# Loading the last tile in two halves and storing it in pieces of 4, 2, 1 and 1 rows

## The chip, the cores and the metric

The kernel runs on one NeuronCore of one Trainium2 chip. The metric is device time in microseconds (us), the median of several executions.

## The reference

`x` has the shape (32, 512, 2048), float32. The last axis is split in two halves of 1024, and the result is gelu(first half) times second half, float32:

```python
half_dim = x.shape[-1] // 2
x1, x2 = (x[..., :half_dim].copy(), x[..., half_dim:].copy())
gelu_x1 = 0.5 * x1 * (1 + erf(x1 / np.sqrt(2)))
return (gelu_x1 * x2).astype(np.float32)
```

That is 134.22 MB read and 67.11 MB written, with little arithmetic per byte.

## The kernel before

The 16384 rows are cut into 16 tiles of 128 partitions x 8 rows. ACT (ScalarE) applies gelu in place to one row per partition, DVE (VectorE) multiplies it into an output tile. Two input and two output buffers rotate. Loads go through the queue of the sync engine (SP), stores through ACT's queue, except those of the last tile, which go through SP's queue in four pieces of two rows, so that storing can begin before all eight rows are done.

```python
R = 8
x_t = x_flat.rearrange("(n p r) d -> n p r d", p=P, r=R)
o_t = out_flat.rearrange("(n p r) d -> n p r d", p=P, r=R)
...                                           # cut: pools with bufs=2 each
def load(i):
    x_tile = xpool.tile([P, R, dim], x.dtype, name="x_tile")
    nc.sync.dma_start(out=x_tile, in_=x_t[i])
    return x_tile

ahead = [load(0), load(1)]
for i in range(n_tiles):
    x_tile = ahead.pop(0)
    o_tile = opool.tile([P, R, half], out.dtype, name="o_tile")
    last = i == n_tiles - 1
    pieces = 4 if last else 1
    step = R // pieces
    for k in range(pieces):
        for r in range(k * step, (k + 1) * step):
            ...                               # cut: gelu on ACT, multiply on DVE
        rows = slice(k * step, (k + 1) * step)
        queue = nc.sync if last else nc.scalar
        queue.dma_start(out=o_t[i][:, rows, :], in_=o_tile[:, rows, :])
    if i + 2 < n_tiles:
        ahead.append(load(i + 2))
```

## Time and profile before

| | before |
|---|---|
| time, median of 3 runs | 472.24 us (471.88 to 472.3) |
| span of the profiled run | 470.3 us |
| DVE / ACT busy | 31% / 26% |
| bytes moved, mean rate | 201.35 MB, 428 GB/s |

These lines are from the page of the kernel before: busy time by engine, then the DMA rows of the 40-slice picture (a 9 is 90% or more), then the chain of work that ended last, by line.

```profile
DVE 146.7 (31%) x128; ACT 124.2 (26%) x129; POOL 0.2 (0%) x4
...
DMA  8999999999999999999999999999999999999998
...
DMA x_tile<-in_x_dram 81%; DVE o_tile L55 15%; ACT x_tile L52 2%; DVEq L90 0%; SPq L40 0%; ACTq L52 0%
...
out_dram<-o_tile SPq DMA_DIRECT2D x4, 1024.0 KB, 5.6
```

The DMA engines are busy from the first slice to the last; the compute engines are idle most of the time. The last line, from the list of DMA issues, says that the four pieces of the last tile took 5.6 us from issue to landing, in the median.

Now the tail. The first fence is the timeline from 450 us (start, length, engine, operation; in brackets the idle time before it and what ended it). The second is the table of stretches (the stretch and its length, busy time of DVE, ACT and POOL, then the granted clock, the mean busy share of the 16 DMA engines, GB/s). Transfers are counted where they start, so a short stretch can show a share a little above 1 or below it.

```profile
453.23 7.68 ACT L52 ACTIVATE x_tile<-x_tile 128x1024 f32<-128x1024 f32 x8 [21.34 <-DMA x_tile<-in_x_dram]
454.32 9.17 DVE L55 TENSOR_TENSOR o_tile<-x_tile 128x1024 f32<-128x1024 f32 x8 [19.85 <-ACT x_tile L52]
456.70 7.14 SPq L62 DMA_DIRECT2D out_dram<-o_tile  x4
```

```profile
452.00:456.00 4.00, 1.68 (x2) 2.77 (x3) 0.00 (x0) 1.00 0.97 418
456.00:458.00 2.00, 2.00 (x3) 2.00 (x4) 0.00 (x0) 1.00 1.07 422
458.00:462.00 4.00, 4.00 (x4) 2.91 (x4) 0.00 (x0) 1.00 0.89 348
462.00:466.00 4.00, 1.49 (x2) 0.00 (x0) 0.00 (x0) 1.00 1.01 428
```

The last load lands, then ten microseconds of ACT and DVE work follow, with stores trickling out behind. The DMA engines stay full while that compute runs.

The records of single packets in the trace show why. A packet is one partition's contiguous run: 64 KB for a full load (median 2.418 us), 32 KB for a full store (1.213 us), 8 KB for a two-row piece (0.309 us). While both queues have work, each of the 16 DMA engines alternates between a load packet and a store packet. (The records don't name the engine, but a packet that starts where another ends can be matched to it. Of the 85 packets that start between 424 and 434 us, 76 have a clear successor, and it is always of the other queue.) When the last load's final packets end, the store of the tile before still has packets until 459.0, and the pieces follow at once until 469.0.

### The profile page before, as it was taken

Reading aid. Unit: us, or ns where it says so; the run is one execution under the profiler, and the core shown is the slowest. Engines: PE = TensorE matmul, PEld = TensorE weight load, DVE = VectorE, ACT = ScalarE, POOL = GpSimd, SP = SyncE. Lnnn points to the kernel's source line nnn. Section 1 sums busy time; section 2 is a strip of 40 time slices with the busy share of each in tenths; the row PEclk is TensorE's granted clock in tenths of the full one; section 3 lists DMA queues with packets and bytes.
Section 4 is the critical chain, followed back from the end, with each engine's and each line's share of the span. In section 5 each row is a group of like instructions: output and inputs, shape, how many; then the busy total and the mean of one; then the engine's idle time right before and its main releaser. Section 6 shows DMA issues by size and latency. Waiting matters only on the chain.

```text
span 470.3 us, 408 instructions
## 1 busy us (share of the span) xinstructions
DVE 146.7 (31%) x128; ACT 124.2 (26%) x129; POOL 0.2 (0%) x4
## 2 busy tenths in 40 slices
DVE  0070704307042070520606116060250702407034
ACT  1050605106050150601406024060330603206042
POOL 0000000000000000000000000000000000000000
DMA  8999999999999999999999999999999999999998
GB/s 357 446 446 382 429 443 424 463 404 443 426 446 421 443 415 449 413 443 424 457 429 435 438 438 415 426 438 435 440 440 418 449 438 435 424 443 432 418 410 351
DMA packets 5042, 201.35 MB, mean 428 GB/s; under 512 B 560, under 2 KB 560, under 8 KB 560
## 3 DMA queue, kind: packets, MB, share of 16 engines
q1 hardware_dynamic: 2880, 138.41, 68.4%
q10 hardware_dynamic: 2160, 62.92, 31.0%
q14 instruction: 2, 0.02, 0.0%
HBM read 134.22 MB, written 67.11 MB: 428 GB/s over the span
## 4 chain that ended last, share of the span: by engine, by line
DMA 81%; DVE 15%; ACT 2%; DVEq 0%; issue 0%; SPq 0%; ACTq 0%
DMA x_tile<-in_x_dram 81%; DVE o_tile L55 15%; ACT x_tile L52 2%; DVEq L90 0%; SPq L40 0%; ACTq L52 0%
## 5 line engine op out<-in xcount | busy, mean ns | idle before, releaser
L55 DVE TENSOR_TENSOR o_tile<-x_tile 128x1024 f32<-128x1024 f32 x128 | 146.7, 1218 | 316.8 <-ACT x_tile L52 316.8
L52 ACT ACTIVATE x_tile<-x_tile 128x1024 f32<-128x1024 f32 x128 | 122.9, 1042 | 336.0 <-DMA x_tile<-in_x_dram 336.0
L52 ACT ACT_TABLE_LOAD x1 | 1.3, 1283 | 0.7 <-PEq L79 0.7
L79 POOL MEMSET const-bfloat16-1.0<- 128x1 bf16 x1 | 0.1, 102 | 0.0
L79 POOL MEMSET const-uint8-127<- 128x1 uint8 x1 | 0.1, 102 | 0.0
L79 POOL MEMSET const-float32-1.0<- 128x1 f32 x1 | 0.1, 99 | 0.0
L79 POOL MEMSET const-float32-0.0<- 128x1 f32 x1 | 0.1, 98 | 0.2 <-issue 0.2
## 6 DMA issues: line engine op xcount, KB each, us to landing
out_dram<-o_tile ACTq DMA_DIRECT2D x15, 4096.0 KB, 39.4
out_dram<-o_tile SPq DMA_DIRECT2D x4, 1024.0 KB, 5.6
x_tile<-in_x_dram SPq DMA_DIRECT2D x16, 47.6
```

Of the source, the lines that this page charges most:

```text
L52: nc.scalar.activation(out=x_tile[:, r, :half], in_=x_tile[:, r, :half], func=GELU)
L55: nc.vector.tensor_mul(out=o_tile[:, r, :], in0=x_tile[:, r, :half], in1=x_tile[:, r, half:],)
L79: nc = _bacc.Bacc("TRN2", target_bir_lowering=False, num_devices=1)
```

## The change

Its intent: rows 0 to 3 of the last tile can be computed and issued while rows 4 to 7 are still arriving, so less work follows the last landing, and the very last store is only one row.

```diff
     def load(i):
         x_tile = xpool.tile([P, R, dim], x.dtype, name="x_tile")
-        nc.sync.dma_start(out=x_tile, in_=x_t[i])
+        parts = 2 if i == n_tiles - 1 else 1
+        for k in range(parts):
+            rows = slice(k * R // parts, (k + 1) * R // parts)
+            nc.sync.dma_start(out=x_tile[:, rows, :], in_=x_t[i][:, rows, :])
         return x_tile
...
-        pieces = 4 if last else 1
-        step = R // pieces
-        for k in range(pieces):
-            for r in range(k * step, (k + 1) * step):
+        cuts = [4, 6, 7, 8] if last else [8]
+        begin = 0
+        for end in cuts:
+            for r in range(begin, end):
...
-            rows = slice(k * step, (k + 1) * step)
+            rows = slice(begin, end)
             queue = nc.sync if last else nc.scalar
             queue.dma_start(out=o_t[i][:, rows, :], in_=o_tile[:, rows, :])
+            begin = end
```

## The prediction

> **What bounds the kernel now.** The page has the DMA engines nine tenths busy in every slice, 428 GB/s; DVE is busy 31%, ACT 26%. The chain of waits is 81% input loads. In the packet records of the trace a load runs as one 64 KB packet per partition (2.42 us each), a full store as 32 KB packets (1.21 us), a two-row piece as 8 KB packets (0.309 us). Each of the 16 engines takes load and store packets strictly in turn, so loads get two thirds. The Trainium skill says so ("DMA: Bandwidth & Descriptors", Queues, rings and completion order: round robin between queues, a whole packet at a time); the trace agrees: 10.03 MB of loads to 5.14 MB of stores between 400 and 435 us.
>
> **The tail before.** The last load lands at 453.14. ACT and DVE (1.15 us a row) work until 463.49; pieces are issued every 2.3 us from 456.70. These 17 us are not idle: the last tile but one still has store packets on each engine until about 458.5, and the pieces follow without a gap at 427 GB/s until 468.9. The span ends at 470.3. So after 453 us the tail is bound by bytes, not by the landing.
>
> **What the change does.** No byte is removed. One load issue is added (0.33 us of the sync queue, hidden). Rows 0 to 3 (5.7 us of ACT and DVE) move ahead of the second half's landing. It also halves the last load's packets to 32 KB, so I expect loads to get a half instead of two thirds while stores are queued. The first half then lands near 443, but the second near 459, six microseconds later than the whole tile now; the store of the last tile but one lands near 457 instead of 459.4. The four-row piece is computed by 449 but waits in the same queue behind the second half; it then gives 2.1 MB, 4.9 us, of cover from 458.5. The next piece needs landing, one ACTIVATE, two DVE rows and issue to first packet (about 1.2 us): 459.2 + 1.1 + 2.3 + 1.3 = about 464, when the cover has just run out: an idle gap of 0.5 to 1 us. The 4 KB packets of the one-row pieces cost 0.16 us each by estimate (half of 0.309). Data should end near 469.2 instead of 468.9.
>
> **On the critical path.** The compute taken from the tail (5 us) is already covered by DMA work: the gain is nil, the loss a small gap, 0.3 us.
>
> **Prediction.** 472.5 us, range 471.5 to 473.5. Faster by over 2%: 0.005; within 2%: 0.99; slower by over 2%: 0.005.
>
> **What would show each step.**
> - Turn-taking: between 424 and 440 us the DMA view has about equal megabytes on both queues.
> - The second half lands at 458 to 460 in the timeline (ACT's last four rows start there).
> - DVE's last row ends near 465, later than now.
> - DMA busy until 469, with at most one short dip near 464.
>
> **What would make it wrong.** If engines shared by bytes, or kept two to one with smaller packets, the second half would land near 453, no gap would appear, and the end could be 0.3 us earlier. If issue to first packet took 2 us for the late pieces, the gap would grow and cost 1 us. Slower one-row packets move the end by tenths. Nothing here reaches 2%.

## The result, and the profile after

A ratio is the mean time of one kernel's fast runs over that of the other's of the same rounds, so it is not quite the ratio of the medians quoted.

| | before | after |
|---|---|---|
| median, first comparison | 472.27 us (4 runs) | 472.74 us (4 runs, 472.41 to 473.45) |
| ratio, 95% interval | | 1.0012 (0.9995 to 1.003) |
| span of the profiled run | 470.3 us | 471.3 us |

There is no gain, and no loss that the interval can tell from nothing. These are the page's lines after:

```profile
DVE 146.9 (31%) x128; ACT 124.3 (26%) x129; POOL 0.2 (0%) x4
...
DMA  8999999999999999999999999999999999999997
...
out_dram<-o_tile SPq DMA_DIRECT2D x1, 2048.0 KB, 17.2
out_dram<-o_tile SPq DMA_DIRECT2D x1, 1024.0 KB, 3.9
out_dram<-o_tile SPq DMA_DIRECT2D x2, 512.0 KB, 4.1
```

The timeline and the stretches after, as above:

```profile
442.21 3.90 ACT L56 ACTIVATE x_tile<-x_tile 128x1024 f32<-128x1024 f32 x4 [9.26 <-DMA x_tile<-in_x_dram]
443.30 4.63 DVE L59 TENSOR_TENSOR o_tile<-x_tile 128x1024 f32<-128x1024 f32 x4 [7.77 <-ACT x_tile L56]
447.96 18.56 SPq L66 DMA_DIRECT2D out_dram<-o_tile  x4
460.31 3.90 ACT L56 ACTIVATE x_tile<-x_tile 128x1024 f32<-128x1024 f32 x4 [14.21 <-DMA x_tile<-in_x_dram]
461.40 4.63 DVE L59 TENSOR_TENSOR o_tile<-x_tile 128x1024 f32<-128x1024 f32 x4 [13.47 <-ACT x_tile L56]
```

```profile
458.00:462.00 4.00, 0.60 (x1) 1.69 (x2) 0.00 (x0) 1.00 0.93 397
462.00:466.00 4.00, 4.00 (x4) 2.21 (x3) 0.00 (x0) 1.00 0.63 266
```

The intent was met in one respect: rows 0 to 3 are done at 447.93 and only four rows follow the last landing. But that landing moved from 453.1 to 460.3 us. (In this profile the whole chain was already 1.06 us late when the last load was issued, at 406.56 instead of 405.50, before anything changed; the repeat below is without that.) The four-row piece, issued at 447.96, needed 17.2 us to land, because it lies in the same queue behind the second half of the load. And the DMA engines now have a hole: share 0.63 between 462 and 466, where it was 1.01.

Why the landing moved is seen in the bytes per queue between 424 and 434 us. The columns are packets, MB, and share of the 16 engines' time; q1 is SP's queue (here loads), q10 is ACT's (stores). First before, then after:

```profile
q1 hardware_dynamic: 44, 2.88, 66.5%
q10 hardware_dynamic: 41, 1.34, 31.1%
```

```profile
q10 hardware_dynamic: 74, 2.42, 56.1%
q1 hardware_dynamic: 66, 2.10, 48.5%
```

Before, loads got two thirds; after, about a half. The half-tile load has 32 KB packets, as the store has, and the engines take turns by packets. The total did not change; the load merely arrives later, and the store that runs beside its first half earlier: that of the last tile but two lands at 437.3 instead of 444.9 us. All 138 data packets that start in these ten microseconds after the change are followed by one of the other queue.

### The profile page after: what moved, and what is told of

It reads as the page before. It is cut to its first block, busy times and chain, and to the rows that moved or that the text cites. A ratio compares the mean times of both kernels' runs of the same rounds, so it can differ in the third digit from the quotient of the medians.

```text
span 471.3 us, 411 instructions
## 1 busy us (share of the span) xinstructions
DVE 146.9 (31%) x128; ACT 124.3 (26%) x129; POOL 0.2 (0%) x4
## 4 chain that ended last, share of the span: by engine, by line
DMA 78%; DVE 14%; another core or an unknown queue 3%; ACT 3%; DVEq 0%; issue 0%; SPq 0%; ACTq 0%
DMA x_tile<-in_x_dram 78%; DVE o_tile L59 14%; ACT x_tile L56 3%; DVEq L95 0%; SPq L44 0%; ACTq L56 0%
## 6 DMA issues: line engine op xcount, KB each, us to landing
out_dram<-o_tile SPq DMA_DIRECT2D x1, 2048.0 KB, 17.2
```

## The experiments

The theory: (1) the tail is bound by bytes, so compute after the landing costs nothing as long as the DMA engines have something queued; (2) smaller load packets shift the turn-taking and delay the second half; (3) after that landing, the queued four-row piece covers about 4.9 us, and the next piece's packets come about then or a little later, which leaves a hole. Rivals: the compute after the landing is on the path after all; small pieces or the extra DMA cost time in themselves; the difference is chance.

"Idle" in this section is worked out from the packet records: the length of a stretch less the summed packet durations in it divided by 16 engines. Recorded packets overlap slightly, so a full stretch comes out a little below zero. Four columns for each run: idle from 450 to 466 us, idle from 466 us to the last data, time of the last data (all us, one profile each), and the median time with the number of timed runs.

```
                idle 450-466   idle 466-end   last data   median (runs)
before             -0.11           0.32         469.0     472.27 (4)
after               1.42           0.02         469.9     472.74 (4)
r_again             0.63           0.03         469.2     472.24 (5)
a_load_only         0.93           0.06         469.5     472.36 (5)
b_store_only        1.66           0.02         470.2     473.29 (5)
c_two_to_one       -0.13           1.07         469.4     472.04 (5)
d_one_row          -0.14           0.65         469.0     472.16 (5)
l_four_four         2.70           0.23         471.2     474.17 (5)
h_fast_tail        -0.12           0.62         469.0     472.19 (5)
k_seven_rows       -0.05           0.45         466.7     469.79 (5)
e_both             -0.17           0.98         469.3     472.17 (5)
```

The kernel before was timed beside each group, on the same chip: median 472.31 us for r, a, b and c; 472.35 for d, h, k and l; 472.32 for e. The three groups ran on three chips, so runs of different groups are compared by their ratio to the kernel before. The profiled execution is not always a typical one: that of a_load_only and that of c_two_to_one were the slowest of their five.

### r_again: the changed kernel once more

No edit.

> The changed kernel again, to narrow its interval beside the others. My theory (bytes bound, plus an idle gap of the DMA engines of about 1.4 us on average after the second half's landing): 0.5 to 1.0 us above the kernel before, gap seen again between 462.5 and 465. Rival (the difference is chance between runs): 0 within 0.3 us, and no stable gap.

Measured: 472.24 us beside 472.31, ratio 0.9999 (0.9987 to 1.0012). The expected 0.5 to 1.0 us of loss did not appear; in the time, chance within 0.3 us is the better reading, and the 0.47 us of the first comparison must not be called a measured loss. The hole is there again, but smaller. ACT starts the last four rows at 459.61. The stretches 458 to 462 and 462 to 466:

```profile
458.00:462.00 4.00, 1.30 (x2) 2.39 (x3) 0.00 (x0) 1.00 0.97 414
462.00:466.00 4.00, 3.33 (x3) 1.51 (x2) 0.00 (x0) 1.00 0.81 336
```

In the first profile the last load packet ended between 456.7 and 459.9 us depending on the engine; here between 458.0 and 459.2. The landing waits for the slowest engine, while the idle is on the engines that were done first. So a run in which the engines have drifted further apart has the larger hole. a_load_only, below, lies between the two (456.9 to 459.7 us, idle 0.93). That is read from three profiles, not tested.

### h_fast_tail: is the compute after the landing on the path?

The kernel before, with a wrong result.

```diff
-                nc.scalar.activation(
-                    out=x_tile[:, r, :half], in_=x_tile[:, r, :half], func=GELU
-                )
+                if last and r % 2 == 0:
+                    nc.scalar.activation(
+                        out=o_tile[:, r, :], in_=x_tile[:, r, :half], func=GELU
+                    )
+                    continue
+                if not last:
+                    nc.scalar.activation(
+                        out=x_tile[:, r, :half], in_=x_tile[:, r, :half], func=GELU
+                    )
```

> The kernel before, with a wrong result on purpose: in the last tile even rows are only activated on ACT and odd rows only multiplied on DVE, so the eight rows take about 5 us instead of 10.3 after the landing. My theory (the tail is bound by bytes): pieces are issued every 1.2 us from about 454.5, all are queued early, the end moves by less than 0.3 us. Rival (the compute after the last landing is on the critical path, which the change set out to shorten): 5 us earlier, ratio 0.989.

The timeline shows that the compute did shrink, and the list of DMA issues shows what became of it:

```profile
453.57 3.90 ACT L53 ACTIVATE o_tile<-x_tile 128x1024 f32<-128x1024 f32 x4 [21.37 <-DMA x_tile<-in_x_dram]
453.58 4.63 DVE L61 TENSOR_TENSOR o_tile<-x_tile 128x1024 f32<-128x1024 f32 x4 [18.81 <-DMA x_tile<-in_x_dram]
454.89 5.08 SPq L68 DMA_DIRECT2D out_dram<-o_tile  x4
```

```profile
out_dram<-o_tile SPq DMA_DIRECT2D x4, 1024.0 KB, 9.0
```

DVE ends at 458.21 instead of 463.49, over five microseconds sooner, and the time is 472.19 us beside 472.35, ratio 0.9998 (0.9984 to 1.0012). What the compute gave up, the pieces spent waiting in the queue: 9.0 us from issue to landing instead of 5.6. The rival's 5 us are excluded: the interval leaves at most 0.8 us. Even this much less compute after the landing, about what the change set out to save, is worth nothing here that these runs can resolve.

### k_seven_rows: do bytes count?

The kernel before; the last load brings seven rows, and row 7 is computed from row 6 (wrong).

```diff
-        nc.sync.dma_start(out=x_tile, in_=x_t[i])
+        rows = slice(0, 7 if i == n_tiles - 1 else R)
+        nc.sync.dma_start(out=x_tile[:, rows, :], in_=x_t[i][:, rows, :])
...                                # cut: ACT and DVE read row 6 for row 7
```

> The kernel before, with a wrong result on purpose: the last load brings 7 of 8 rows, and row 7 is computed from row 6, so compute and stores stay and 1.05 MB of load go. My theory (bytes bound): 1.05 MB at 433 GB/s, that is 2.4 us earlier, less 0.3 to 1 us if the compute after the landing then starts to show. Rival (latency of the compute chain after the landing alone): the landing itself comes earlier by as much, so this run tells only together with the fast tail run; bytes bound needs 2 us here and nothing there.

Measured: 469.79 us beside 472.35, ratio 0.9948 (0.9936 to 0.9961): 2.56 us between the medians. The 1.05 MB left out take 2.4 us at 433 GB/s (16 engines, 64 KB in 2.418 us). With the run before, this settles the first point: taking away compute gave nothing, taking away bytes gave their full time.

### a_load_only and b_store_only: each half of the change alone

```diff
 # a_load_only, against the changed kernel
-        cuts = [4, 6, 7, 8] if last else [8]
+        cuts = [2, 4, 6, 8] if last else [8]
```

> Load in halves kept, stores in four pieces of two rows as before. My theory: second half lands at 459 to 460 as in the changed kernel, two pieces wait behind it and give the same 4.9 us of cover, the third is issued at the same time as the changed kernel's second, so the gap of 1.4 us stays; end within 0.2 us of the changed kernel. Rival (the small pieces of 4 KB and 16 KB packets cost the time): back to the time of before, 0.5 us or more faster than the changed kernel.

Measured: 472.36 us, ratio to before 0.9998 (0.9985 to 1.001), beside 472.24 for the changed kernel in the same rounds. The second half lands late again (ACT starts at 460.06) and the hole stays, 0.93 us. So late landing and hole come from the split of the load, not from the small pieces. Undoing the small pieces did not make it faster.

```diff
 # b_store_only, against the changed kernel
-        parts = 2 if i == n_tiles - 1 else 1
+        parts = 1
```

> Whole load kept, stores in 4, 2, 1 and 1 rows. My theory: load lands at 453.1 as before; the first piece is issued only after four rows, at about 458.9, its packets start at 460.1, while the earlier store has run out at 458.5: a gap of about 1.6 us, end 1.2 us later than before. Rival (only packet sizes count): 0.1 us later than before, no gap.

Measured: 473.29 us beside 472.31, ratio 1.0019 (1.0007 to 1.0032): 0.98 us slower between the medians. The hole sits earlier:

```profile
458.00:462.00 4.00, 4.00 (x5) 3.12 (x4) 0.00 (x0) 1.00 0.60 250
462.00:466.00 4.00, 1.70 (x2) 0.00 (x0) 0.00 (x0) 1.00 0.93 389
```

The first piece is issued at 459.19, after four rows; its packets begin at 460.0, when the store of the tile before has run dry. This is the only part of the change with a loss clear of noise. Put together with the split load, the loss is gone within the noise (472.24 us for the changed kernel in the same rounds): the four-row piece then is ready long before it is needed.

### c_two_to_one: the turn-taking

The change kept; the two stores that run beside the last load are issued as two halves each, in 16 KB packets, so that load and store packets are two to one again.

```diff
             queue = nc.sync if last else nc.scalar
-            queue.dma_start(out=o_t[i][:, rows, :], in_=o_tile[:, rows, :])
+            halves = 2 if i in (n_tiles - 3, n_tiles - 2) else 1
+            for h in range(halves):
+                hr = rows if halves == 1 else slice(h * R // 2, (h + 1) * R // 2)
+                queue.dma_start(out=o_t[i][:, hr, :], in_=o_tile[:, hr, :])
```

> The change kept; the stores of the two tiles before the last are each issued as two halves of 4 rows (16 KB packets), so that packets of the last load and of the stores stand again at two to one. My theory (turn-taking by packets): the second half lands near 453 to 455 instead of 460, stores still have work then, no gap over 0.4 us, end about 1 us earlier than the changed kernel, equal to before within 0.3. Rival (a second load DMA as such delays the landing): landing stays near 460, gap and time as in the changed kernel.

The bytes per queue between 424 and 434 us, then the timeline of the last four rows:

```profile
q1 hardware_dynamic: 95, 3.11, 72.0%
q10 hardware_dynamic: 96, 1.31, 30.6%
```

```profile
447.55 4.63 DVE L59 TENSOR_TENSOR o_tile<-x_tile 128x1024 f32<-128x1024 f32 x4 [14.31 <-DMA out_dram<-o_tile]
452.01 3.90 ACT L56 ACTIVATE x_tile<-x_tile 128x1024 f32<-128x1024 f32 x4 [10.58 <-DMA x_tile<-in_x_dram]
```

Only the store's packets were made smaller, and the load has more than two thirds again; the second half lands at about 452.0 although the load is still two DMAs. The rival (the extra DMA delays it) is out. The hole is gone. A side effect: the first four rows on DVE now waited for an output buffer, because the store that held it got the smaller share and landed only at 447.3. That cost nothing, since the DMA engines were full.

The time is 472.04 us, ratio to before 0.9991 (0.9978 to 1.0005), 0.20 below the changed kernel's median. I had expected about 1 us below it. The table of idle shows where it went: with the hole filled, the engines do not all end together. The idle after 466 us rose from 0.03 to 1.07 us. In the changed kernel the early engines wait in the hole for the same issue and finish together; without it, the ones ahead finish early and the slowest one still sets the end. So a hole of 0.6 us was partly drift that would have been idle at the end anyway. This is read from one profile of each kernel; the differences in time are within the noise.

### d_one_row and l_four_four: the hole made smaller and larger

```diff
 # against the changed kernel: d_one_row, then l_four_four
-        cuts = [4, 6, 7, 8] if last else [8]
+        cuts = [4, 5, 6, 7, 8] if last else [8]
+        cuts = [4, 8] if last else [8]
```

> The changed kernel with the four late rows stored one by one, so that the first piece after the second landing is one row instead of two. My theory (the cover of 4.9 us from the four-row piece runs out before the next piece's packets come): the first late packets come 1.15 us earlier, so the idle of the engines between 458 and 466 falls from 0.6 to 1.4 us to 0.3 or less, end 0.3 to 1 us earlier than the changed kernel in the same call's terms (ratio to before about 0.999). Rival (extra small DMAs cost time by themselves): later than the changed kernel by 0.1 us or more.

> The changed kernel with the late half stored as one piece of four rows. My theory: its packets come at landing 459.6 to 460.3 plus 1.1 + 4.6 + 1.2, about 466.5 to 467.2, the cover ends at 463.0 to 463.5, so the idle of the engines is about 3.2 us instead of about 1, and the end comes about 2 us later than the changed kernel (ratio to before 1.004 to 1.006). Rival (the idle gap is hidden by something else): within 0.5 us of the changed kernel.

The stretch from 462 to 466 us, first of d_one_row, then of l_four_four:

```profile
462.00:466.00 4.00, 3.25 (x3) 1.43 (x2) 0.00 (x0) 1.00 0.96 399
```

```profile
462.00:466.00 4.00, 3.23 (x3) 1.40 (x2) 0.00 (x0) 1.00 0.22 94
```

In both, the landing is where the changed kernel has it (ACT starts at 459.53 and 459.51), so only the piece that follows the cover differs. With one row it is in time: its packets begin at 462.8 and the hole is gone. With four rows it is issued at 465.26, its packets begin at 466.1, and the engines stand still in between. The times are 472.16 us (ratio 0.9998, 0.9986 to 1.0011) and 474.17 us (ratio 1.0045, 1.0032 to 1.0058). The long hole costs 1.8 us between the medians; this and b_store_only show that such a hole is paid for in time. Filling the small one brought back nothing that these runs can resolve, as in c_two_to_one: idle after 466 us rose to 0.65. Five small DMAs instead of four cost nothing visible either.

### e_both: is there anything to win?

c_two_to_one and d_one_row together.

> Both cures at once: two-to-one packets as in c_two_to_one and the late rows stored one by one. My theory: no gap after the landing, but no byte less, so no better than the kernel before beyond 0.3 us (ratio 0.999 to 1.000). Rival (some gain of the split was only hidden by the gap and adds up when both causes of the gap are gone): ratio 0.997 or lower.

Measured: 472.17 us beside 472.32, ratio 0.9998 (0.9984 to 1.0012). No version that moves the same bytes was faster than the kernel before by more than the noise.

## Why the prediction was right

- *The tail is bound by bytes, not by the landing.* Right. Over 5 us less compute after the landing changed nothing (0.9998), 1.05 MB less gave 2.56 us. The Trainium skill names the ceiling ("Perfetto Trace Analysis", Engine Utilization: a single core is bounded by its 16 DMA engines, about 435 GB/s in sum); this trace agrees, with 428 GB/s over the whole span.
- *The engines take turns by packets, so halving the packets slows the load.* Right: 2.88 to 1.34 MB became 2.10 to 2.42, and shrinking the store's packets gave 3.11 to 1.31 and brought the landing back from 459.6 to 452.0. My check was badly chosen, though: over 424 to 440 us the queues were not equal (4.19 MB of loads, 2.88 of stores). From about 436 to 439 no store packet ran, and the load had the engines alone. The earlier store had finished sooner, at 435.7; the next was issued at 435.56, but its first packet came at 439.1. Why so late is not shown: in the repeat the next store was issued at 434.45, before the earlier one ended at 436.2, and there was still a pause until 438.1.
- *Second half near 459.2.* 460.3 in the first profile, 459.6 in the repeat; the first was 1.06 us late already before the last load was issued. DVE's last row ended at 466.0 and 465.3, against "near 465". The store of the last tile but one, forecast to land near 457 instead of 459.4, landed at 459.5 in the first profile, so no earlier than before, and at 457.6 in the repeat.
- *Cover of 4.9 us, the next piece too late, a hole of 0.5 to 1 us.* The mechanism was right. The size is 0.6 us in one profile and 1.4 in the other; I had reckoned with one time for all engines, but they end the load up to 3 us apart, and the early ones wait for the landing of the last.
- *Small packets cost about half of 0.309 us each.* Right: 0.159 us in the trace for 4 KB.
- *Gain nil, loss 0.3 us.* The gain was nil. The 0.3 us is neither confirmed nor refuted: 0.47 us between the medians at first, -0.07 in the repeat. That 472.74 lies so near the forecast 472.5 is partly luck; the range of 471.5 to 473.5 would have held b_store_only (473.29) and the unchanged kernel as well, so it is the runs above that test the mechanism. The prediction did not say why a hole of 0.5 to 1 us should cost only 0.3, and my expectation for r_again (0.5 to 1.0 us of loss) was too simple: it let the hole add about its length to the time. By the table of idle, part of what it costs comes back at the end, where the engines then finish together.

The skill gives the general rule for such a change ("Perfetto Trace Analysis", DMA Optimizations: splitting a DMA may let the task finish sooner "if DMA engines are generally idle"). Here the condition fails, and so does the gain.

## What to carry to other kernels

Before shortening a tail, look at whether the DMA engines are idle in it: compute after the last landing is free while older transfers are still queued, and only fewer bytes help. When two queues share the DMA engines, compare their contiguous runs per partition: here these set each queue's share (64 against 32 KB, 32 against 32, 32 against 16), so splitting a load can make the load slower and a neighbouring store faster. Hand the engines their next small piece before the queue runs dry; the size of the first piece after a landing decides that.

## What the Trainium skill lacked or had wrong

- "DMA: Bandwidth & Descriptors", Queues, rings and completion order, says that engines go round robin by packets, but not what follows for the shares. Here a packet was one partition's contiguous run (64 or 32 KB for loads, 32 to 4 KB for stores), and halving one queue's runs moved its bytes from 2.88 against 1.34 MB to 2.10 against 2.42 in 10 us.
- The same page, Rules for kernel authors, warns of small transfers and asks for 1 MiB or more per DMA. It does not say what small ones cost when they are queued back to back. Here that was little: 0.5 MB pieces ran at 410 GB/s (d_one_row, 465 to 468 us), beside 421 GB/s for 1 MB pieces in the kernel before in the same stretch. By the median packets, 4 KB in 0.159 us is 412 GB/s over 16 engines, 8 KB in 0.309 us is 424, and 64 KB in 2.418 us is 434.
- The same page, Where 436 GB/s comes from, says without a condition that about 358 GB/s binds transfers between HBM and SBUF. This kernel, on one core, moved 428 GB/s over 470 us; the page's own remark one section earlier, that each core gets about 358 when both stream, and the note in "Perfetto Trace Analysis", Engine Utilization, that a single active core can go beyond the share, fit better. What the other core of the pair did is not in the record.
- No page that I found says how far the 16 engines drift apart within one load: their last packets ended 2.2 us apart before the change and 1.2 to 3.2 us apart after it, which is as large as the hole studied here.
